# Attention maxima as two 64-row matmuls into a double bank, column-tiled sums, and a fixed VectorE order

## The chip, the cores and the metric

The kernel runs on one core of a Trainium2 chip. The metric is the device time in microseconds (us) of one execution, lower is better. A core has five engines that work in parallel, each through its own queue in order: TensorE (PE in the profile; PEld is its weight load), VectorE (DVE), ScalarE (ACT), GpSimd (POOL), and SyncE (SP), which here issues the transfers. TensorE writes into PSUM, which has 8 banks of 128 partitions by 512 floats; VectorE and ScalarE read it from there.

## What is computed

One layer of a transformer block on 2048 tokens of width 1024, with 256 context tokens. The part that the change touches is the attention: 8 query heads of 64 columns, 2 key/value heads (four query heads share one), and 2304 keys (256 context, 2048 latent) for every query.

```
def attend(q, k, v):
    s = jnp.einsum('bkgqd,bknd->bkgqn', q, k, preferred_element_type=jnp.float32)
    p = jax.nn.softmax(s, axis=-1).astype(v.dtype)
    return jnp.einsum('bkgqn,bknd->bkgqd', p, v)
```

Around it stand an input projection with norms and rotary tables, a gated MLP branch, a merge of the two branches with an output projection, and a squared-ReLU MLP.

## The kernel before, in words

The stages run one after another: the input projection (`project`, to about 782 us of the trace), the attention (`attend`, 782 to about 1545 us), the merge, and the MLP (`ffn`).

**Units.** `attend` (L890) goes over 16 units, one for each of 4 blocks of 512 queries and 4 pairs of heads. In a unit it goes over 18 key tiles of 128 keys in 3 groups of 6; the text calls them g0, g1 and g2, with key tiles j0 to j5, j6 to j11, j12 to j17. For each key tile `scores` (L810) makes the transposed scores of the two heads: two matmuls per head (L815, L816) into one bank, of 512 columns each, and an Exp on ScalarE (L818) into an SBUF tile. L815 multiplies the rounded queries with the keys (128 rows: the high and the low part of the keys). L816 adds the low part of the queries and, through a row of ones in `KB`, minus the maximum of the query. After the six key tiles of a group `values` (L821) is called for the six tiles of the group before it, so each group's values come one group later: two matmuls per key tile, one per head, each into its own 64 partitions of one bank `o` (L826, 64 weight columns; in the records each of these float32 matmuls appears as two instructions). The same function adds the exponentials up for the softmax sums, 8 additions of a unit on VectorE and the rest on GpSimd (L841).

**Maxima.** The maximum of a query must be known before its unit begins. `attn_prep` (L747) of the next unit is a generator that `attend` advances three times per key tile. It transposes the queries (L754, copied by L758), makes for each head, each of four 128-query tiles and each of five key blocks (one of 256 and four of 512 keys) one matmul into one bank (L770) and one maximum on VectorE (L774), 40 of each in a unit; then the maximum over the blocks (L779), its negative into the tile `pb` (L780), and the transposes of `pb` (L789, in the trace under the helper's line L161), which the next unit's L816 needs. `attn_load` (L731) fetches the queries of the unit after that and splits them (L740 to L742).

**Sums.** When a unit is over, `sums` (L844) adds the partial sums of GpSimd and VectorE (L846) and stores the unscaled output. `finish` (L853) then makes the row sums with 8 matmuls of one column (L858), 16 instructions in the records, a reciprocal (L863), a transpose (L866), and stores the result. `br_inputs` (L945) of the merge reads these reciprocals back, spread over 64 partitions, and multiplies (L962).

**Other work in the stage.** `mod_rest` (L273) goes over 32 weight tiles in 36 steps: each loads a tile and multiplies and adds on VectorE (L283, L287), and every ninth ends with some matmuls (L299, L315). `br_inputs(0)`, called `late` in `attend`, is handed out in the last unit, one step per key tile.

**What sets the order.** The source order is a priority; a scheduler at compile time places each engine's instructions by readiness in its own model. Two lists restrict it, both through `order` (L1393): the steps of `mod_rest` in `attend` are pinned on all engines to their place in the source, and TensorE's whole order in `attend` is that of the source (`pe_pins`). VectorE, ScalarE, GpSimd and SyncE may otherwise be reordered. PSUM is one pool of 8 banks for the whole kernel (L168); a bank is taken for each score tile, maximum, transpose and sum, and `o` holds one for most of a unit.

Of the kernel before, what the change touches and what calls it, by code (L numbers as in the profile page):

```python
# [9 lines left out]
F32 = mybir.dt.float32  # L10
# [51 lines left out]
class Kern:  # L62
    def __init__(self, ctx, tc, I, out):
# [5 lines left out]
        self.pe_pins = []  # L69
        self.open_pools, self.pool_of = {}, {}  # L70

# [91 lines left out]
    def constants(self):  # L163
# [4 lines left out]
        self.psp = ec(self.tc.tile_pool(name="ps", bufs=8, space=PSUM))  # L168
# [26 lines left out]
        def operands(n):  # L195
# [535 lines left out]
    def attn_load(self, b, p):  # L731
# [8 lines left out]
        nc.gpsimd.memset(pb[:, :, :, HD:], 0.0)  # L740
        nc.scalar.copy(pa, qt.unsqueeze(3).broadcast_to([P, TT, 2, 2, HD]))
        nc.vector.tensor_tensor(  # L742
            out=pb[:, :, :, :HD], in0=qt, in1=f32(pa[:, :, :, 0, :]), op=ALU.subtract
# [3 lines left out]
    def attn_prep(self, b, p, loaded, out):  # L747
# [17 lines left out]
        for h in range(2):  # L765
            for t in range(TT):
                for c, ka in enumerate(self.KA):
                    n = CTX if c == 0 else TB
                    ps = self.bank([TB])
                    nc.tensor.matmul(  # L770
                        ps[:, :n], qa[h][:, t * P : (t + 1) * P], ka[kv][:, :n],
                        start=True, stop=True,
                    )
                    nc.vector.tensor_reduce(  # L774
                        out=mx[:, t, h, c : c + 1], in_=ps[:, :n], axis=AX.X, op=ALU.max
                    )
                    yield
# [3 lines left out]
            out=pb[:, :, :, HD : HD + 1], in0=nm.unsqueeze(3), scalar1=-1.0, scalar2=None,  # L781
# [14 lines left out]
    def attn_steps(self, b, p, qab):  # L796
# [56 lines left out]
        def finish():  # L853
            sm = self.bank([2 * TT])
            for h in range(2):
                for t in range(TT):
                    c = h * TT + t
                    nc.tensor.matmul(  # L858
                        sm[:, c : c + 1], accs[1][h][:, t * P : (t + 1) * P],
                        self.ones[:, :1], start=True, stop=True,  # L860
                    )
            r = self.small([2 * TT])
# [27 lines left out]
    def attend(self, qabs, prep0, loaded, side, late):  # L890
# [5 lines left out]
        for i, u in enumerate(units):  # L896
# [4 lines left out]
            for g in range(0, NKT, GROUP):  # L901
# [14 lines left out]
                for f in pend:  # L916
                    f()
# [539 lines left out]
```

## Time and profile before

| what | us |
|---|---|
| median of 3 runs (lowest, highest) | 3280.03 (3278.81, 3280.11) |
| the profiled execution, its own time | 3275.92 |
| its span, first to last instruction | 3274.1 |
| attention: first score matmul of the first unit to that of the last (15 units) | 782.2 to 1499.9 |
| last unit, to its last value matmul | 1499.9 to about 1540 |

The profile is of one execution. A row of a list of groups gives the line, the engine, the operation, what it writes and reads, the shapes and the count; then the busy time and the mean duration of one; then the idle time ahead of it and what ended that. A row of a timeline gives start, duration, engine, line and, in brackets, the idle time before it and the instruction that ended it; `x3` means three merged instructions. TensorE is pipelined: a matmul of 512 columns lasts about 0.39 us in the records, but the next one starts before it ends, so the cost of one is the step from start to start. A row of a table by stretch gives the stretch and its length, the busy time of each engine with its number of instructions, the granted TensorE clock (1.00 is full), the share of DMA time, and GB/s.

### The profile page before, as it was taken

To read this page: it belongs to the slowest core of one execution; us is meant where nothing else is said; L and a number is where in the kernel's file an instruction comes from. 1 tells how busy PE (TensorE), PEld (TensorE's weight loads), DVE (VectorE), ACT (ScalarE), POOL (GpSimd) and SP (SyncE) were. 2 spreads that over 40 slices of the span, in tenths; PEclk is the share of its full clock that TensorE was granted. 3 is DMA by queue.
4 is the path that set the end of the run, shared out by engine and by line. 5 is a ranking of instruction groups with operands and counts; after the bars stand their busy time and mean duration, and the time that the engine had idled before them with its cause. 6 is when DMAs were issued, how large, how long until landed. Compare 5 with 4: busy or idle time off the path is not lost.

```text
span 3274.1 us, 38611 instructions
## 1 busy us (share of the span) xinstructions
PE 3127.4 (96%) x14100; PEld 2397.0 (73%) x14100; DVE 1987.0 (61%) x2910; ACT 1353.3 (41%) x2034; POOL 982.9 (30%) x672
## 2 busy tenths in 40 slices
PE   8999999999999999998799988999999899999999
PEld 4888887887555666664587766888778688888777
DVE  4736354556787888774433339887754676664555
ACT  3343534343444544453322216444543344443333
POOL 1423233334777887777633310000000000000000
PEclk9999999999999999999899998999999999999999
DMA  6353534342111111001555536989655634445564
GB/s 201 98 193 107 169 118 152 114 139 83 49 49 52 46 33 52 26 11 43 183 177 173 163 111 228 313 308 312 220 202 197 220 137 158 145 149 195 209 218 170
DMA packets 331838, 484.79 MB, mean 148 GB/s; under 512 B 33920, under 2 KB 166144, under 8 KB 331648
## 3 DMA queue, kind: packets, MB, share of 16 engines
q1 hardware_dynamic: 326032, 481.98, 44.0%
q8 instruction: 110, 1.80, 0.2%
q10 hardware_dynamic: 5616, 0.35, 0.1%
q14 instruction: 80, 0.66, 0.1%
HBM read 347.97 MB, written 134.28 MB: 147 GB/s over the span
## 4 chain that ended last, share of the span: by engine, by line
PE 76%; DVE 10%; DMA 5%; POOL 3%; issue 3%; ACT 2%; SPq 1%; ACTq 0%; DVEq 0%; POOLq 0%
PE b L1176 11%; PE b L1177 11%; PE b L1175 11%; PE b L157 7%; PE b L156 7%; PE b L155 7%; PE b L826 7%; PE b L770 4%; PE b L815 3%; PE b L816 3%; DVE ts L774 2%; PE b L161 2%; DMA f<-w2o_d 1%; DMA w<-in_w_in 1%; DVE f L1270 1%
## 5 line engine op out<-in xcount | busy, mean ns | idle before, releaser
L774 DVE TENSOR_REDUCE ts<-b 128x1 f32<-128x512 f32 (+1 forms) x640 | 357.4, 627 | 153.5 <-PE b L770 153.3
L841 POOL TENSOR_TENSOR t<-t,pt 128x512 f32<-128x512 f32 x272 | 376.5, 1410 | 137.2 <-ACT pt L818 134.6
L1261 DVE TENSOR_TENSOR f<-f,f 128x1024 fp32r<-128x1024 f32 x224 | 272.8, 1224 | 235.1 <-ACT f L1260 230.7
L1260 ACT CAST f<-f 128x1024 fp32r<-128x1024 f32 x224 | 235.0, 1051 | 381.8 <-DMA f<-ao_d 287.7
L1176 PE MATMUL b<-f,f 128*128 128x512 f32 x896 | 354.1, 395 | 15.2 <-DVE f L1261 14.7
L1177 PE MATMUL b<-h,f 128*128 128x512 f32 x896 | 350.0, 391 | 9.1 <-DVE f L1132 7.2
L1175 PE MATMUL b<-h,f 128*128 128x512 f32 x896 | 350.3, 392 | 4.8 <-ACT f L1131 4.3
L818 ACT ACTIVATE pt<-b 128x512 f32<-128x512 f32 x480 | 257.9, 603 | 227.0 <-PE b L816 221.7
L1177 PE MATMUL b<-f,f 128*128 128x512 f32 x896 | 351.1, 392 | 0.0
L1176 PE MATMUL b<-h,f 128*128 128x512 f32 x896 | 349.9, 391 | 0.0
L1175 PE MATMUL b<-f,f 128*128 128x512 f32 x896 | 306.6, 396 | 22.2 <-ACT f L1260 20.6
L127 POOL TENSOR_TENSOR w<-w,w 128x1024 fp32r<-128x1024 f32 x60 | 146.8, 2447 | 388.3 <-ACT w L123 152.0
L815 PE MATMUL b<-t,t 128*128 128x512 f32 x576 | 238.1, 413 | 0.0
L816 PE MATMUL b<-t,t 128*128 128x512 f32 x576 | 226.8, 394 | 0.0
L826 PE MATMUL b<-pt,t 128*64 128x512 f32 x960 | 223.3, 613 | 0.0
L123 ACT CAST w<-w 128x1024 fp32r<-128x1024 f32 x120 | 125.9, 1049 | 225.7 <-DMA w<-in_w_in 197.9
L1175 PEld LDWEIGHTS b<-f,f 128*128 128x128 f32 x896 | 168.7, 190 | 64.5 <-ACT f L1260 26.0
L1176 PEld LDWEIGHTS b<-f,f 128*128 128x128 f32 x896 | 169.8, 189 | 59.8 <-DVE f L1261 25.0
L155 PE MATMUL b<-t,w 128*128 128x512 f32 x512 | 203.2, 397 | 1.0 <-DVE t L568 1.0
L1177 PEld LDWEIGHTS b<-h,f 128*128 128x128 f32 x896 | 169.0, 189 | 45.9 <-DVE f L1132 7.9
L157 PE MATMUL b<-t,w 128*128 128x512 f32 x512 | 200.6, 392 | 0.0
L156 PE MATMUL b<-t,w 128*128 128x512 f32 x512 | 200.6, 392 | 0.0
(212 smaller groups left out, 6249.4 us busy)
## 6 DMA issues: line engine op xcount, KB each, us to landing
w<-in_w_in SPq DMA_DIRECT2D x120, 512.0 KB
ao_d<-f SPq DMA_DIRECT2D x224, 256.0 KB
f<-ao_d SPq DMA_DIRECT2D x112, 512.0 KB
f<-w2o_d SPq DMA_DIRECT2D x112, 512.0 KB
f<-in_w_ff SPq DMA_DIRECT2D x48, 1024.0 KB
w2o_d<-f SPq DMA_DIRECT2D x112, 256.0 KB
t<-in_w_mod SPq DMA_DIRECT2D x32, 512.0 KB
f<-x_d SPq DMA_DIRECT2D x64, 256.0 KB
```

Of the source, the lines that this page charges most:

```text
L155: mm(ps, sh, mh, start=start, stop=False)
L156: mm(ps, sh, ml, start=False, stop=False)
L157: mm(ps, sl, mh, start=False, stop=stop)
L774: nc.vector.tensor_reduce(out=mx[:, t, h, c : c + 1], in_=ps[:, :n], axis=AX.X, op=ALU.max)
L815: nc.tensor.matmul(s, self.KA[c][kv][:, ks], qa[h], start=True, stop=False)
L816: nc.tensor.matmul(s, self.KB[c][kv][:, ks], qb[h], start=False, stop=True)
L826: nc.tensor.matmul(o[0][h * HD : (h + 1) * HD, :], self.V[c][:, i, kv * HD : (kv + 1) * HD], pts[j][h], start=j == 0, stop=j == NKT - 1,)
L841: engs[e].tensor_tensor(out=accs[e][h], in0=first, in1=pt, op=ALU.add)
L1175: mm(ps, wh, hh, start=start and k == 0, stop=False, skip_group_check=True)
L1176: mm(ps, wh, hl, start=False, stop=False, skip_group_check=True)
L1177: mm(ps, wl, hh, start=False, stop=k == len(w) - 1, skip_group_check=True)
L1261: nc.vector.tensor_tensor(out=l, in0=f32(l), in1=f32(h), op=ALU.subtract)
```

## The change

Seven things are altered, all in or around `attend`.

1. The two heads' maxima are two matmuls of 64 rows, in rows 0 to 63 and 64 to 127 of the array, each into one half of a tile of two banks, `bb`. Both use only the high part of the keys; for that the halves of `KB` and of `pb` change places, so that the high part of the keys lies in rows 64 to 127 as well. One VectorE instruction takes both maxima: 20 of 2x512 or 2x256 numbers instead of 40.
2. The maxima come in bursts of two pairs, every fourth step of the generator, so 10 bursts in a unit. At three steps per key tile they stand behind j1, j3, j4 and j5, then j7, j8, j9 and j11, then j12 and j13.
3. PSUM in the attention is 4 single banks and 2 double ones; before and after it, 8 single ones. In the first unit's preparation, which runs within the projection, the pairs use two single banks and two maxima.
4. The sums are two matmuls with 64 columns of ones as weights and the 512 sums as moving operand, one for each half of the partitions; the row is copied by ScalarE and stored. After the fourth pair of heads of a block one transfer reads all 32 rows of 128 sums back, one reciprocal is taken, and one transfer stores it.
5. `finish` runs behind the values of g0 (that is, at the end of g1) and g1 instead of in the midst of the scores.
6. The steps of `mod_rest` move from behind j2, j8 and j14 to the ends of g0 and g2, with a second step at each in every fourth unit; `attn_load` moves from j11 to the end of g1. None is pinned.
7. VectorE's order in `attend` is that of the source, as TensorE's is (`fixed`).

```diff
--- before.py
+++ after.py
@@ -111,11 +112,28 @@
     def small(self, shape, dtype=F32):
         return self.sb("fs" if "back" in self.open_pools else "ts", shape, dtype)
 
-    def bank(self, shape, dtype=F32):
+    def psum(self, banks):
+        if self.banks:
+            self.psum_stack.close()
+        self.banks = banks
+        self.psum_stack = ExitStack()
+        self.psp = self.psum_stack.enter_context(
+            self.tc.tile_pool(name="ps", bufs=1, space=PSUM, reuse_waits="tile")
+        )
+
+    def bank(self, shape, dtype=F32, tag="b"):
         self.uid += 1
-        t = self.psp.tile([P] + list(shape), dtype, tag="b", name=f"b_{self.uid}")
-        self.tags[t.name] = "b"
+        t = self.psp.tile(
+            [P] + list(shape), dtype, tag=tag, name=f"{tag}_{self.uid}", bufs=self.banks[tag]
+        )
+        self.tags[t.name] = tag
         return t
+
+    def pair(self):
+        if "bb" in self.banks:
+            t = self.bank([2, TB], tag="bb")
+            return t, [t[:, i] for i in range(2)]
+        return None, [self.bank([TB]) for _ in range(2)]
 
     def split(self, src, hi, lo, hi_eng="act", lo_eng="pool"):
         nc = self.nc
...
@@ -203,13 +221,8 @@
 
         self.ao_d = [operands(f"ao{blk}") for blk in range(2)]
         self.wo_d = operands("w2o")
-        self.rs_d = [
-            [
-                dp.tile([2 * TT, P], F32, tag=f"rs{b}_{p}", name=f"rs_d{b}_{p}")
-                for p in range(NH // 2)
-            ]
-            for b in range(NB)
-        ]
+        self.sm_d = spill("sm", [NH, TB])
+        self.rs_d = spill("rs", [NH, TB])
         self.open("base")
         self.open("front")
 
...
@@ -762,23 +775,32 @@
         yield
         kv = p // 2
         mx = self.small([TT, 2, len(self.KA)])
-        for h in range(2):
-            for t in range(TT):
-                for c, ka in enumerate(self.KA):
-                    n = CTX if c == 0 else TB
-                    ps = self.bank([TB])
+        for t in range(TT):
+            tok = slice(t * P, (t + 1) * P)
+            for c, (ka, kb) in enumerate(zip(self.KA, self.KB)):
+                n = CTX if c == 0 else TB
+                both, ps = self.pair()
+                for h, (rows, k) in enumerate(((slice(0, HD), ka), (slice(HD, P), kb))):
                     nc.tensor.matmul(
-                        ps[:, :n], qa[h][:, t * P : (t + 1) * P], ka[kv][:, :n],
-                        start=True, stop=True,
+                        ps[h][:, :n], qa[h][rows, tok], k[kv][rows, :n], start=True, stop=True
                     )
+                if both is not None:
                     nc.vector.tensor_reduce(
-                        out=mx[:, t, h, c : c + 1], in_=ps[:, :n], axis=AX.X, op=ALU.max
+                        out=mx[:, t, :, c : c + 1], in_=both[:, :, :n], axis=AX.X, op=ALU.max
                     )
-                    yield
+                else:
+                    for h in range(2):
+                        nc.vector.tensor_reduce(
+                            out=mx[:, t, h, c : c + 1], in_=ps[h][:, :n], axis=AX.X,
+                            op=ALU.max,
+                        )
+                if (t * len(self.KA) + c) % 2:
+                    for _ in range(4):
+                        yield
         nm = self.small([TT, 2])
         nc.vector.tensor_reduce(out=nm, in_=mx, axis=AX.X, op=ALU.max)
         nc.vector.tensor_scalar(
-            out=pb[:, :, :, HD : HD + 1], in0=nm.unsqueeze(3), scalar1=-1.0, scalar2=None,
+            out=pb[:, :, :, 0:1], in0=nm.unsqueeze(3), scalar1=-1.0, scalar2=None,
             op0=ALU.mult,
         )
         for _ in range(6):
...
@@ -851,38 +873,42 @@
             nc.sync.dma_start(self.at_d[b][p * P : (p + 1) * P, :], oc)
 
         def finish():
-            sm = self.bank([2 * TT])
+            sm = self.bank([TB])
             for h in range(2):
-                for t in range(TT):
-                    c = h * TT + t
-                    nc.tensor.matmul(
-                        sm[:, c : c + 1], accs[1][h][:, t * P : (t + 1) * P],
-                        self.ones[:, :1], start=True, stop=True,
-                    )
-            r = self.small([2 * TT])
-            nc.vector.reciprocal(r, sm)
+                nc.tensor.matmul(
+                    sm[h * HD : (h + 1) * HD, :], self.ones[:, :HD], accs[1][h],
+                    start=True, stop=True,
+                )
+            row = self.t2([TB])
+            nc.scalar.copy(row, sm)
+            for h in range(2):
+                nc.sync.dma_start(
+                    self.sm_d[b][2 * p + h : 2 * p + h + 1], row[h * HD : h * HD + 1]
+                )
+            if p + 1 == NH // 2:
+                n = NH * TT
+                r = self.t1([P])
+                pack = lambda d: d.rearrange("h (t c) -> (h t) c", c=P)
+                nc.sync.dma_start(r[:n], pack(self.sm_d[b]))
+                yield
+                nc.vector.reciprocal(r[:n], r[:n])
+                nc.sync.dma_start(pack(self.rs_d[b]), r[:n])
             yield
-            rt = self.bank([P])
-            nc.tensor.transpose(rt[: 2 * TT], r, self.ident)
-            rr = self.t1([P])
-            nc.scalar.copy(rr[: 2 * TT], rt[: 2 * TT])
-            nc.sync.dma_start(self.rs_d[b][p], rr[: 2 * TT])
-            yield
 
         return scores, values, sums, finish
 
     def kb_build(self):
         nc = self.nc
         z = self.t2([TB])
-        nc.gpsimd.memset(z[HD:], 0.0)
-        nc.gpsimd.memset(z[HD : HD + 1], 1.0)
+        nc.gpsimd.memset(z[:HD], 0.0)
+        nc.gpsimd.memset(z[0:1], 1.0)
         for c, KA in enumerate(self.KA):
             n = TB if c else CTX
             KB = []
             for ka in KA:
                 kb = self.t2([TB], F32R)
-                nc.vector.tensor_copy(kb[:HD, :n], f32(ka[:HD, :n]))
-                nc.scalar.copy(kb[HD:, :n], z[HD:, :n])
+                nc.vector.tensor_copy(kb[HD:, :n], f32(ka[:HD, :n]))
+                nc.scalar.copy(kb[:HD, :n], z[:HD, :n])
                 KB.append(kb)
                 yield
             self.KB.append(KB)
...
@@ -903,18 +929,18 @@
                     scores(j)
                     for _ in range(3):
                         next(prep, None)
-                    if j % 6 == 2:
-                        at = self.here()
-                        next(side, None)
-                        self.pins.append(range(at, self.here()))
-                    if j in (GROUP + 4, 2 * GROUP + 1):
-                        next(after, None)
-                    if j == 11 and i + 2 < len(units):
-                        loaded.append(self.attn_load(*units[i + 2]))
                     if i + 1 == len(units):
                         next(late, None)
                 for f in pend:
                     f()
+                if g:
+                    next(after, None)
+                if g == GROUP and i + 2 < len(units):
+                    loaded.append(self.attn_load(*units[i + 2]))
+                else:
+                    next(side, None)
+                    if i % 4 == 0:
+                        next(side, None)
                 pend = [lambda v=values, j=j: v(j) for j in range(g, g + GROUP)]
             for _ in prep:
                 pass
...
@@ -928,7 +954,7 @@
             pass
         for _ in side:
             pass
-        self.pe_pins.append(range(begin, self.here()))
+        self.fixed.append(range(begin, self.here()))
 
     def load_w_out(self):
         nc = self.nc
...
@@ -990,6 +1015,7 @@
         for _ in start:
             pass
         self.close("mid", "base")
+        self.psum({"b": 8})
         self.open("join")
         steps = [(b, m) for b in range(NB) for m in range(KC)]
         it = iter(steps)
...
@@ -1379,7 +1405,10 @@
 
         prep0 = tail()
         self.project(prep0)
+        for _ in prep0:
+            pass
         self.close("front")
+        self.psum({"b": 4, "bb": 2})
         self.open("mid")
         self.open("pre", side="right")
         first = {}
...
@@ -1403,7 +1433,7 @@
                 if n in self.tags and n not in seen:
                     seen.add(n)
                     keys.append(self.tags[n])
-            held = idx in pinned or (idx in pe and i.engine == tensor)
+            held = idx in pinned or (idx in fixed and i.engine in engines)
             after = keys + ([i.engine] if held else [])
             for prev in {last[k].name for k in after if k in last}:
                 self.tc.add_manual_dep(i, prev, dep, reason="order")
```

Left out: the halves in `attn_load` exchanged in the same way as in `kb_build`, the reads of `rs_d` in `br_inputs` in the new layout, the first `self.psum({"b": 8})`, and the renaming in `__init__`.

More of the change, by code (lines that the diff above doesn't have):

```diff
@@ L68, in __init__ @@
         self.pins = []
-        self.pe_pins = []
+        self.fixed = []
         self.open_pools, self.pool_of = {}, {}
+        self.banks = None
     def here(self):
@@ L1390, in build @@
         self.close("back")
+        self.psum_stack.close()
         self.order()
```

17 lines of the change are left out of this document (8 added, 9 removed).

## The prediction

> **What bounds the kernel now.** I read the page first, then the table by stretches, the groups of the attention stage, and TensorE's timeline start by start.
>
> ```profile
> span 3274.1 us, 38611 instructions
> ...
> PE 3127.4 (96%) x14100; PEld 2397.0 (73%) x14100; DVE 1987.0 (61%) x2910; ACT 1353.3 (41%) x2034; POOL 982.9 (30%) x672
> ...
> PE   8999999999999999998799988999999899999999
> ...
> DVE  4736354556787888774433339887754676664555
> ...
> PEclk9999999999999999999899998999999999999999
> ```
>
> TensorE is busy nearly everywhere; in the attention, slices 10 to 19, VectorE is at 70 to 80% beside it. Where TensorE is full, time is won only by taking work or waits from it. The stage by stretches (columns: PE, PEld, DVE, ACT, POOL, clock):
>
> ```profile
> 782.20:1499.90 717.70, 701.87 (x3255) 433.98 (x3253) 578.10 (x830) 347.47 (x651) 551.87 (x401) 0.98 0.13 41
> ...
> 1408.90:1454.40 45.50, 45.26 (x219) 28.61 (x217) 34.17 (x53) 22.96 (x43) 34.68 (x27) 1.00 0.04 13
> ```
>
> The first row is 15 units: 47.85 us each. The second is one unit with no `mod_rest` step at full clock: 45.5 us, so TensorE's own work. The difference, 717.7 - 15 x 45.5 = 35.2 us, is other matmuls and lost time. So two questions decide: what the change does to the 45.5, and how much of the 35.2 goes.
>
> The groups of the stage:
>
> ```profile
> L774 DVE TENSOR_REDUCE ts<-b 128x1 f32<-128x512 f32 x480 | 301.2, 680 | 111.4 <-PE b L770 111.3
> L841 DVE TENSOR_TENSOR t<-t,pt 128x512 f32<-128x512 f32 x80 | 99.5, 1243 | 13.4 <-ACT pt L818 11.4
> L841 DVE TENSOR_TENSOR t<-pt,pt 128x512 f32<-128x512 f32 x32 | 53.6, 1676 | 0.0
> L287 DVE SCALAR_TENSOR_TENSOR t<-t,silu,t 128x1024 f32<-128x1024 f32 x28 | 50.6, 1808 | 0.0
> L774 DVE TENSOR_REDUCE ts<-b 128x1 f32<-128x256 f32 x120 | 49.7, 414 | 28.9 <-PE b L770 28.9
> L858 PE MATMUL b<-ones,t 128*128 128x1 f32 x240 | 28.3, 248 | 0.0
> L841 DVE TENSOR_TENSOR t<-t,t 128x512 f32<-128x512 f32 x16 | 12.9, 807 | 0.7
> L299 PE MATMUL b<-t,ones 128*128 128x512 f32 x8 | 3.8, 592 | 0.0
> L315 PE MATMUL b<-ones,t 128*128 128x1 f32 x32 | 3.7, 245 | 0.0
> ```
>
> **TensorE's part of a unit.** The steps from start to start:
>
> ```profile
> 1417.62 0.63 PE L770 MATMUL b<-t,t 128*128 128x512 f32 x2
> 1418.18 1.08 PE L826 MATMUL b<-pt,t 128*64 128x512 f32 x4
> ...
> 1422.52 1.03 PE L826 MATMUL b<-t,t 128*64 128x512 f32 x4
> 1423.48 0.50 PE L815 MATMUL b<-t,t 128*128 128x512 f32 x1
> 1423.81 0.39 PE L816 MATMUL b<-t,t 128*128 128x512 f32 x1
> ...
> 1426.70 0.39 PE L815 MATMUL b<-t,t 128*128 128x512 f32 x1
> 1426.92 0.39 PE L816 MATMUL b<-t,t 128*128 128x512 f32 x1
> ...
> 1427.60 0.73 PE L770 MATMUL b<-t,t 128*128 128x512 f32 x3
> 1428.18 0.40 PE L815 MATMUL b<-t,t 128*128 128x512 f32 x1
> ```
>
> A step of 512 columns is 0.23 us (1426.70 to 1426.92), a key tile's four score matmuls 0.92. The three L770 from 1427.60, one of 256 columns, take 0.58 = 0.23 + 0.11 + 0.23. So the 40 maxima of a unit take 32 x 0.227 + 8 x 0.113 = 8.2 us. Taken two at a time they are 20 steps: **-4.1 us**. That two such tiles run together is seen here for 64-column tiles: the four L826 from 1422.52 end after 1.03, two steps of 0.43 with two instructions in each.
>
> Against it stands the change of mode. From full to 64 columns: the last L770 starts at 1417.85, the first L826 at 1418.18, which is 0.33 where 0.23 is usual, and the next pair starts 0.05 late (four end after 1.08, not 1.03): 0.15 us. Back: the last pair starts at 1422.95, L815 at 1423.48, 0.52 where 0.43 is usual, and L816 comes 0.33 after it, not 0.23: 0.21 us. No row shows 64-row tiles. The bounds are 0 and this; I take this, the only change of mode that the trace has. Ten bursts cost 10 x 0.36 = 3.6, less 2 x 0.21 where a burst ends a group (behind j5 and j11) and values follow anyway: **+3.2 us**. So most of what pairing wins goes into the modes. The Trainium skill (TensorEngine Tiling (Array Packing), Key Properties) states that changing the tiling mode drains the TensorE; the trace agrees, with 0.10 us lost at each of the two changes before the weight load comes on top.
>
> The sums: 16 one-column instructions (28.3 / 240 x 16 = 1.9 us) become 4 in two steps of 0.43, right behind the values in the same mode: **-1.0 us**. In total -1.9 us.
>
> **VectorE and the two double banks.** VectorE's maximum lasts 0.680 for 512 numbers and 0.414 for 256, so 1.04 ns per number: 1.21 us for 2x512 (estimate). In a row they overlap by (480 x 0.680 - 301.2) / 480 = 0.05, so one comes every 1.16. Two double banks hold two pairs, so a burst's second pair waits for the second maximum of the burst before.
>
> ```profile
> 1204.59 0.85 PE L770 MATMUL b<-t,t 128*128 128x512 f32 x3
> ...
> 1205.02 5.21 DVE L774 TENSOR_REDUCE ts<-b 128x1 f32<-128x512 f32 x9 [1.66 <-PE b L770]
> ```
>
> From first matmul to first maximum is 0.43. So the second maximum is over 0.43 + 1.16 + 1.21 = 2.80 us after the burst's first matmul, and handing the bank back takes 0.14 at most (818.76 to 818.90 in a row below), of which I take half. TensorE, with one key tile between, wants the bank 0.23 + 0.23 + 0.21 + 0.92 + 0.15 + 0.23 = 1.97 after it. The wait of 0.9 occurs three times in a unit, behind j4, j8 and j13, where two full pairs lie one key tile back (elsewhere there are two key tiles between, or a short pair): **+2.7 us**. Eight banks hid this before.
>
> Four single banks, one of them `o`:
>
> ```profile
> 1500.70 5.01 ACT L818 ACTIVATE pt<-b 128x512 f32<-128x512 f32 x10 [5.33 <-PE b L816]
> ```
>
> ScalarE makes one exponential per 0.49 us (10 in 5.01), TensorE one score tile per 0.46. Behind j14 to j17, without maxima between, TensorE loses 8 x 0.03: **+0.2 us** (0 to 0.6). A unit comes to 45.5 - 1.9 + 2.7 + 0.2 = 46.5 us; 15 of them: **+15 us**.
>
> **What goes of the 35.2 us.** L299 and L315 are 7.5 us and stay. The other 27.7 are waits and half-clock stretches:
>
> ```profile
> 818.90 1.94 PE L161 MATMUL b<-ident,t 128*128 128x128 f32 x8 [3.00 <-DVE t L780]
> ```
> ```profile
> 976.68 0.62 ACT L123 CAST in<-raw 128x512 fp32r<-128x512 f32 x1 [7.74 <-DVE raw L962]
> ...
> 978.81 0.58 PE L770 MATMUL b<-t,t 128*128 128x256 f32 x1 [2.31 <-ACT t L758]
> ```
> ```profile
> 1146.00:1149.40 3.40, 3.18 (x22) 2.66 (x22) 3.40 (x7) 1.22 (x3) 3.40 (x3) 1.00 0.00 0
> 1149.40:1152.80 3.40, 3.40 (x9) 1.07 (x10) 3.40 (x7) 1.09 (x2) 3.32 (x3) 0.50 0.01 2
> ```
>
> The first: an addition was put between L779 and L780, and the transposes of `pb` waited; in source order L780 follows L779. The second: `br_inputs`, meant for the last unit, was moved up; ScalarE waited 7.74 us for VectorE's L962 with the queries' copies behind it. With VectorE's order fixed, L962 cannot come before the last unit. The third: 3.4 us at half clock behind a stretch with the 16 one-column matmuls of L858, which go. I leave 3.4 us for half clock elsewhere: **-24.3 us**.
>
> **What is added at the edges.** First the second `mod_rest` step of every fourth unit.
>
> ```profile
> 1409.96 1.03 PE L161 MATMUL b<-ident,t 128*128 128x128 f32 x8
> 1410.75 0.48 PE L815 MATMUL b<-t,t 128*128 128x512 f32 x1
> ```
>
> On TensorE g0's scores last 6 x 0.92, plus 0.8 for the transposes, plus the bursts with their modes, 0.70, 0.82, 0.70 with a wait of 0.9, and 0.61: 10.1 us from the unit's start; its values, 12 steps of 0.43, and the mode bring it to 15.5. VectorE begins the last two maxima at 9.6 + 0.43 and is free at 12.3; three additions (166.0 / 128 = 1.3 us each) bring it to 16.2, a step of 1.8 to 18.0. The first maximum of g1 is wanted at 15.5 + 2 x 0.92 + 0.1 + 0.43 = 17.9. There is no slack, so the second step adds 0 to 1.8 us; I take 1.0, four times: **+4 us**. In the last unit VectorE has only additions beside `br_inputs`, whose transfers now hold those up in line, 0 to 5 us; I take **+1**. At the end:
>
> ```profile
> 1544.89 0.28 SPq L869 DMA_DIRECT2D rs_d<-t  x1
> 1545.27 0.38 SPq L974 DMA_DIRECT2D bw<-in_w_br_attn  x1
> ...
> 1547.91 0.62 ACT L123 CAST bw<-bw 128x512 fp32r<-128x512 f32 x1 [3.04 <-DMA bw<-in_w_br_attn]
> ```
>
> The merge's loads stand behind the store of the last sums on SP. Now that queue may hold a store, a load and a store in a chain, 0 to 5 us at about 2 us for each that waits for the one before (the load at 1545.27 ended ScalarE's wait at 1547.91); the shorter sums give 1 back: **+1**. The same chain after the three other blocks has g2 to run in. In the projection, streaming and mode cost nearly cancel: 0.
>
> **Sum:** 15 - 24.3 + 4 + 1 + 1 = -3.3 us on the profiled execution's 3275.9, which gives 3272.6. The median of the runs lies 4.1 above that execution, so **3277 us**, 0.1% below 3280.0.
>
> **The rivals.**
>
> *The change of mode is cheap for row tiles* (faster). Then 3.2 us of a unit go, but bursts come 0.36 sooner and each of three waits grows by that: -2.1 us a unit, -32 in all: 3245. For it: nothing measured speaks on row tiles. Against it: both changes in the trace cost. The Trainium skill (TensorE: Matmul & The Clock Gate, Packing small matmuls) says that a weight load overlaps running matmuls only when row groups differ; full and half tiles share rows, so it speaks against this rival too, and no row here tests it.
>
> *VectorE becomes the bound behind the values* (slower). A first maximum of g1 has no slack, so whatever makes VectorE later there is paid by TensorE one for one. Additions vary from 0.81 to 1.68 us by group. If the three ahead of g1 and the step take 0.5 us longer each through GpSimd's load, with nothing free to be moved up in their place, a unit gets 1.5 us longer: +22: 3299. It decides from about 0.8 us per unit on. Against it: the 1.3 us are already a mean over contended ones.
>
> *The pairs do not run at once* (slower; the change would not do what it says). Streaming stays 8.2: +4.1, the three waits shrink by 0.45 each: +2.8 a unit, +42: 3319. Against it: column tiles do run together.
>
> **How the numbers follow.** The forecast has 0.47, cheap modes 0.28, VectorE 0.17, no pairing 0.08. About 0.2% (6.6 us) can be told from no change. The forecast's own range, from the bounds of edges, half clock and banks, is 3263 to 3293: it gives 0.17 to faster, 0.19 to same, 0.11 to slower. With the rivals: faster 0.45, same 0.19, slower 0.36. The range 3238 to 3308 takes in the first two rivals and leaves out the third and some of the first.
>
> **What would show it.** Starts within a pair of L770's successor a few ns apart, or 0.23 (third rival). Steps into and out of a burst 0.15 and 0.21 longer, or not (first rival). Unstalled units of 46.5 us; TensorE waiting for VectorE's maximum about 0.9 us behind j4, j8 and j13; a longer wait at j8 means the second rival. No half-clock stretch where the sums are, and no wait of 2 us for copies or `pb`. The forecast is wrong if a unit lies outside 44 to 48, or if the 27.7 us are not the fixed order's to win.

## The result, and the profile after

The changed kernel takes **3375.24 us** (median of 4 runs, 3372.41 to 3380.28) where the kernel before, beside it, takes 3279.42: a ratio of 1.030, 95% interval 1.028 to 1.032. The forecast was 3277, with a range that ended at 3308. It is wrong in sign and in size.

The page of the changed kernel, the rows that were shown of before:

```profile
span 3375.5 us, 37968 instructions
...
PE 3144.3 (93%) x13892; PEld 2323.0 (69%) x13892; DVE 1981.3 (59%) x2598; ACT 1359.1 (40%) x2034; POOL 990.9 (29%) x672
...
PE   7999999999898989889689996999999999999998
...
PEclk9999999999998989999899997999999999999999
```

No engine has much more to do: VectorE is busy 6 us less than before and TensorE 17 us more, on 208 fewer instructions, part of them at a lower clock. What is new are the 8s and 6s of TensorE in slices 10 to 20, the attention, with dips of the clock beside them. So it looks like waiting, not work.

The changed kernel's 15 units in the table by stretches (us, then PE, PEld, DVE, ACT, POOL, clock, share of DMA, GB/s):

```profile
783.10:1576.30 793.20, 711.60 (x3073) 367.26 (x3073) 544.44 (x506) 349.95 (x644) 553.82 (x399) 0.94 0.10 32
```

They last 793.2 us where the row of before had 717.7, so **+75.5**; VectorE is busy 34 us less and the clock averages 0.94, not 0.98: 0.06 x 793 = 48 us of clock are missing, where 0.02 x 718 = 14 us were missing before. From the first score matmul of the last unit to the first matmul of the merge it is 72.8 us where it was 53.3, **+19.5**. The rest of the kernel adds 6. These two numbers, units and last unit, are what each experiment below is read by.

What TensorE and VectorE wait for (engine, what it needs <- who gives it: total us, times, longest):

```profile
PEld bb L784 <- DVE ts L788: 126.2, 122, 4.5
DVE t L755 <- ACT t L754: 97.4, 13, 7.8
```

TensorE waits for maxima, as long as 4.5 us, and VectorE itself waits 13 times, about 7.5 us each, for ScalarE's cast of the queries in `attn_load`: once in almost every unit. One such place, VectorE's timeline at the end of g1:

```profile
1070.68 1.82 DVE L788 TENSOR_REDUCE ts<-bb 128x2 f32<-128x1024 f32 x2 [0.39 <-PE bb L784]
1072.42 1.12 DVE L863 TENSOR_TENSOR t<-pt,pt 128x512 f32<-128x512 f32 x1
1081.02 1.71 DVE L755 TENSOR_TENSOR t<-t,t 128x512 f32<-128x512 f32 x1 [7.48 <-ACT t L754]
1082.65 4.61 DVE L788 TENSOR_REDUCE ts<-bb 128x2 f32<-128x1024 f32 x4
```

ScalarE and TensorE at the same time:

```profile
1076.98 0.59 ACT L883 COPY t<-b 128x512 f32<-128x512 f32 x1 [6.00 <-PE b L878]
1077.60 1.13 ACT L840 ACTIVATE pt<-b 128x512 f32<-128x512 f32 x2
1079.46 0.60 ACT L840 ACTIVATE pt<-b 128x512 f32<-128x512 f32 x1 [0.73 <-PE b L838]
1079.95 1.04 ACT L754 CAST t<-t 128x1024 fp32r<-128x1024 f32 x1
```
```profile
1077.97 0.73 PE L784 MATMUL bb<-t,t 64*128 64x512 f32 x4
...
1079.43 0.39 PE L838 MATMUL b<-t,t 128*128 128x512 f32 x1
1083.92 0.79 PE L784 MATMUL bb<-t,t 64*128 64x512 f32 x2 [4.10 <-DVE ts L788]
1085.05 0.80 PE L784 MATMUL bb<-t,t 64*128 64x512 f32 x2 [0.34 <-DVE ts L788]
1085.78 0.79 PE L837 MATMUL b<-t,t 128*128 128x512 f32 x1
1086.37 0.63 PE L838 MATMUL b<-t,t 128*128 128x512 f32 x1
```

It reads as a chain. The subtraction L755 stands in the source at the end of g1, so VectorE's fixed order puts it ahead of the maxima of j12 and j13. Its cast L754 is made by ScalarE, whose order is not fixed, behind L883 and three exponentials of g2. L883 is the copy of the row of sums that items 4 and 5 of the change put there; it waits 6.00 us for the values and the sums. The load of the queries had gone out at 1062.00, and no transfer runs from 1066 to 1072, so the trace shows nothing else that kept the cast from running in these 6 us. VectorE waits for it; TensorE's pairs of 1077.97 fill both double banks; the next pair has no bank and TensorE stops for 4.10 us. Then its matmuls last 0.63, not 0.39. The same stretch in the table (after the length: PE, PEld, DVE, ACT, POOL, clock, share of DMA, GB/s):

```profile
1079.60:1083.00 3.40, 0.22 (x1) 0.00 (x0) 1.98 (x2) 1.89 (x3) 3.24 (x4) 0.80 0.74 287
1083.00:1086.40 3.40, 2.14 (x6) 1.10 (x7) 3.40 (x4) 0.00 (x0) 3.32 (x4) 0.50 0.00 0
1086.40:1089.80 3.40, 3.40 (x12) 2.48 (x10) 3.30 (x5) 2.22 (x5) 2.51 (x4) 0.69 0.00 0
```

A stretch with TensorE busy for 0.22 us is followed by half clock (0.50) until 1088.5. The Trainium skill (TensorE: Matmul & The Clock Gate, What's actually happening) says that an idle window of about 3.4 us halves the clock and a busy one restores it; the trace agrees, a wait of 4.10 us and half clock after it. In four of the 13 units the wait is shorter than that, 3.08 to 3.21 us, and half clock follows there as well (0.57 to 0.60 from the end of the wait to the transposes of `pb`).

### The profile page after: what moved, and what is told of

The parts are those of the page before. It is cut to its first block, busy times and chain, and to the rows that moved or that the text cites. A ratio compares the mean times of both kernels' runs of the same rounds, so it can differ in the third digit from the quotient of the medians.

```text
span 3375.5 us, 37968 instructions
## 1 busy us (share of the span) xinstructions
PE 3144.3 (93%) x13892; PEld 2323.0 (69%) x13892; DVE 1981.3 (59%) x2598; ACT 1359.1 (40%) x2034; POOL 990.9 (29%) x672
## 4 chain that ended last, share of the span: by engine, by line
PE 72%; DVE 12%; DMA 6%; POOL 4%; issue 3%; ACT 3%; SPq 1%; ACTq 0%; DVEq 0%; POOLq 0%
PE b L1202 11%; PE b L1203 11%; PE b L1201 11%; PE b L175 7%; PE b L173 6%; PE b L174 6%; PE b L848 6%; PE b L837 4%; PE b L838 3%; DVE ts L788 3%; PE bb L784 2%; PE b L179 2%; DMA f<-w2o_d 1%; DMA w<-in_w_in 1%; DVE f L1296 1%
## 5 line engine op out<-in xcount | busy, mean ns | idle before, releaser
L788 DVE TENSOR_REDUCE ts<-bb 128x2 f32<-128x512 f32 x300 | 318.6, 1112 | 139.8 <-PE bb L784 139.6
L837 PE MATMUL b<-t,t 128*128 128x512 f32 x576 | 268.8, 467 | 4.3 <-ACT pt L840 3.5
L838 PE MATMUL b<-t,t 128*128 128x512 f32 x576 | 242.9, 422 | 0.0
L173 PE MATMUL b<-t,w 128*128 128x512 f32 x512 | 202.9, 396 | 1.5 <-DVE t L581 1.4
L784 PE MATMUL bb<-t,t 64*128 64x256 f32 x600 | 123.8, 466 | 81.6 <-DVE ts L788 81.6
L175 PE MATMUL b<-t,w 128*128 128x512 f32 x512 | 199.8, 390 | 0.0
```

The lines of the kernel that those rows point to most:

```text
L173: mm(ps, sh, mh, start=start, stop=False)
L175: mm(ps, sl, mh, start=False, stop=stop)
L788: nc.vector.tensor_reduce(out=mx[:, t, :, c : c + 1], in_=both[:, :, :n], axis=AX.X, op=ALU.max)
L837: nc.tensor.matmul(s, self.KA[c][kv][:, ks], qa[h], start=True, stop=False)
L838: nc.tensor.matmul(s, self.KB[c][kv][:, ks], qb[h], start=False, stop=True)
```

## The experiments

**Theory after this reading:** the wait of VectorE at L755 is the loss in the units, half clock included; the last unit is longer because `br_inputs` and the chain of the last sums stand ahead of what the merge needs. **Rivals:** the fixed order as such; row tiles or double banks.

All kernels in one table; "units" and "last" are the two stretches named above, from each kernel's trace; "before" is the median of the kernel before, run beside it. From the merge to the end it is 1718 to 1728 us in every kernel.

| kernel | units | last | median | before | ratio (95%) |
|---|---|---|---|---|---|
| before | 717.7 | 53.3 | 3280.03 | | |
| after | 793.2 | 72.8 | 3375.24 | 3279.42 | 1.030 (1.028 to 1.032) |
| sub_late | 714.8 | 72.5 | 3292.83 | 3280.97 | 1.005 (1.003 to 1.006) |
| cast_early | 786.5 | 71.8 | 3361.64 | 3275.24 | 1.027 (1.024 to 1.029) |
| ve_free | 760.2 | 55.8 | 3321.20 | 3280.97 | 1.012 (1.011 to 1.014) |
| before_fixed | 743.6 | 71.4 | 3329.65 | 3280.97 | 1.015 (1.013 to 1.017) |
| sub_late_full | 722.6 | 72.6 | 3303.33 | 3280.97 | 1.007 (1.005 to 1.008) |
| sub_late_loose | 735.2 | 54.7 | 3293.45 | 3275.24 | 1.006 (1.004 to 1.008) |
| loose_chain | 727.8 | 51.5 | 3284.55 | 3275.24 | 1.003 (1.002 to 1.004) |
| loose_banks8 | 692.0 | 59.8 | 3257.43 | 3275.24 | 0.995 (0.993 to 0.997) |
| late_spread | 715.4 | 61.0 | 3281.50 | 3273.81 | 1.002 (1.000 to 1.003) |
| best | 693.9 | 56.6 | 3261.65 | 3273.81 | 0.995 (0.993 to 0.997) |
| best_full | 679.8 | 56.5 | 3249.37 | 3273.81 | 0.991 (0.988 to 0.994) |

### sub_late: only the subtraction moved

```diff
                 if g:
                     next(after, None)
+                if g == 2 * GROUP and i + 2 < len(units):
+                    self.sub()
                 if g == GROUP and i + 2 < len(units):
-                    loaded.append(self.attn_load(*units[i + 2]))
+                    loaded.append(self.attn_load(*units[i + 2], defer=True))
```

`attn_load` loads and casts where it did; its subtraction, now `self.sub`, is issued a group later.

> The changed kernel with one instruction moved: VectorE's subtraction of attn_load (L755) is issued at the end of g2, behind the maxima and the values, instead of at the end of g1; the load, the cast on ScalarE (L754) and the memset stay. Theory (a wait in the fixed order): in the changed kernel L755 stands in VectorE's fixed line ahead of g2's first maxima and waits for ScalarE's L754, which stands behind g2's first exponentials; TensorE waits 4.2 us for the maxima in 13 units, and the clock halves behind that. Then about 13 x 4.3 = 56 us of waits and some 30 us of half clock go: near 3290 us, units of 46 to 48 us. Rival (VectorE's work itself is too much behind the values): the maxima of g2 stay late, units stay above 52 us, time above 3350 us. Rival (modes and double banks): as the first rival, the units stay long but spread over g0 and g1 too.

The units go from 793.2 to 714.8, and the clock comes back:

```profile
783.40:1498.20 714.80, 679.92 (x3072) 341.01 (x3072) 551.49 (x506) 345.14 (x644) 552.81 (x399) 1.00 0.11 35
1211.60:1258.70 47.10, 45.10 (x207) 22.40 (x205) 38.52 (x35) 23.09 (x43) 38.59 (x28) 1.00 0.10 23
```

So one instruction of 1.4 us, placed a group too early, cost 78.4 us in the units, more than their whole loss. Of this, 76.9 us lie in g2 of the 13 units. From g2's first score matmul to the first pair of maxima behind j13 they take 6.1 to 7.1 us where sub_late takes 2.9: 49.5 us in all, the wait. From that pair to the transposes of `pb` they take 7.0 to 8.2 where sub_late takes 5.6: 27.2 us in all, at a granted clock of 0.57 to 0.76. The last unit does not change (72.5), and the kernel is 0.5% slower than the one before, no longer 3%, close to the 3290 expected. What the prediction took for the double banks is seen here as it was priced:

```profile
1074.81 0.40 PE L844 MATMUL b<-t,t 128*128 128x512 f32 x1
1075.17 0.50 PE L790 MATMUL bb<-t,t 64*128 64x512 f32 x2
1076.30 0.39 PE L790 MATMUL bb<-t,t 64*128 64x256 f32 x2 [0.63 <-DVE ts L794]
1076.62 0.50 PE L843 MATMUL b<-t,t 128*128 128x512 f32 x1
```

From 1075.17 to 1076.30 it is 1.13 where a pair takes 0.23: a wait of 0.90, behind j4.

### cast_early: the cast moved ahead instead

```diff
                 if g == GROUP and i + 2 < len(units):
-                    loaded.append(self.attn_load(*units[i + 2]))
-                else:
+                    self.sub()
+                if g == 0 and i + 2 < len(units):
+                    loaded.append(self.attn_load(*units[i + 2], defer=True))
+                if g != GROUP or i + 2 >= len(units):
                     next(side, None)
```

Load and cast stand at the end of g0, the subtraction stays at the end of g1.

> The changed kernel with VectorE's subtraction of attn_load left at the end of g1, but its load, cast (L754 of the changed kernel) and memset issued one group earlier, at the end of g0 (the mod_rest step stays at g0 and g2). Theory (VectorE's line waits for ScalarE's cast): the cast is over before g1 ends, VectorE does not wait, time within 6 us of sub_late (3293). Rival (the place of the subtraction in VectorE's line itself is what costs): it stays above 3350 us. A middle value would say that the cast still slips behind exponentials in some units.

It stays at 3361.64, a miss, and the most useful one. VectorE's timeline at the end of a g0:

```profile
1047.51 1.29 DVE L869 TENSOR_TENSOR t<-t,pt 128x512 f32<-128x512 f32 x2
1055.26 2.40 DVE L300 SCALAR_TENSOR_TENSOR t<-t,silu,t 128x1024 f32<-128x1024 f32 x1 [6.45 <-DMA t<-in_w_mod]
1057.58 2.94 DVE L794 TENSOR_REDUCE ts<-bb 128x2 f32<-128x1024 f32 x3
...
1070.34 1.76 DVE L756 TENSOR_TENSOR t<-t,t 128x512 f32<-128x512 f32 x1
```

The subtraction (L756) no longer waits. But now `mod_rest`'s L300 does, for its weights (64.8 us in 11 waits), which SP issues only at 1051.08, right behind a store of the unit before (L879, 1050.65). A g1 takes 22 to 25 us in these eleven units where it is 16.0 to 16.7 in most of sub_late. Another instruction and another giver, a group earlier, but again in VectorE's line ahead of the maxima, and nearly the same price. So the time is the one that the rival named, but the reason is not. In the two units with an early cast in which L300 does not wait, 3 and 10, the unit is as long as in sub_late (48.8 and 48.9 us): the subtraction in its old place then costs nothing.

### ve_free: only TensorE's order fixed

```diff
-        engines = (self.nc.tensor.engine, self.nc.vector.engine)
+        engines = (self.nc.tensor.engine,)
```

> The changed kernel with only TensorE's order fixed in the attention, as before the change; VectorE may be reordered by the scheduler. Theory (a wait in the fixed order): L755 no longer holds the maxima up, time near 3300 us (the moved-up br_inputs and additions ahead of the transposes may come back and cost some 10 to 20 us of that). Rival (modes and double banks cost the time): it stays above 3350 us.

At 3321.20 it lies between the theory's 3300 and the rival's 3350, and the units are at 760.2. The wait at L755 is gone, and TensorE waits for `pb`, and ScalarE for the transposes of it, far more than in the kernel before (there 5.4 us in 11 waits of PE at L161 for L780):

```profile
ACT t L813 <- PE b L179: 35.5, 18, 3.7
...
PE b L179 <- DVE t L802: 31.0, 13, 3.2
```

The last unit falls to 55.8: with VectorE free, `br_inputs` is again done before it.

### before_fixed: the kernel before with VectorE's order fixed

```diff
-            held = idx in pinned or (idx in pe and i.engine == tensor)
+            held = idx in pinned or (idx in pe and i.engine in engines)
```

> The kernel before with VectorE's order in the attention fixed to the source, and nothing else. Theory (a wait in the fixed order): L742 is issued behind j11's maxima and ahead of g0's additions and g2's maxima, and waits for L741 on ScalarE; it has TensorE's values of 5 us as slack, so it costs from 1 to 4 us a unit, plus half clock, and the last unit is held up by br_inputs as in the changed kernel: 3300 to 3350 us. Rival (the fixed order by itself is harmless or wins the waits that I had put on free order): 3245 to 3280 us.

The fixed order alone makes the kernel before 1.5% slower, and its last unit 71.4 long. The time lies in the range of the theory, but the wait that this named, L742 for L741, has no row in the trace. What the fixed order was to remove, the late `pb`, it makes worse (5.4 us in the kernel before for the first row here):

```profile
PE b L161 <- DVE t L780: 30.9, 11, 3.8
PEld b L161 <- DVE t L780: 27.8, 9, 4.2
...
DVE t L287 <- DMA t<-in_w_mod: 10.8, 7, 2.0
```

In source order `mod_rest`'s step behind j14 stands ahead of L779 and L780. It takes VectorE 1.3 to 2.4 us itself, and in seven units it waits for its weights too. So a fixed order is neither good nor bad; what counts is what stands ahead in it and when its data come.

### sub_late_full: 128 rows in the double banks

```diff
-                        ps[h][:, :n], qa[h][rows, tok], k[kv][rows, :n], start=True, stop=True
+                        ps[h][:, :n], qa[h][:, tok], ka[kv][:, :n], start=True, stop=True
```

> sub_late with the maxima taken by full matmuls of 128 rows (high and low part of the keys, as before the change), one after the other, into the same double banks and with the same single VectorE instruction: no change of mode. By the sum of the prediction the pairing wins 4.1 us of streaming and pays 3.2 to 4 us of modes in a unit, so this is within 1 us a unit of sub_late, 15 us in all, and the waits for the double banks get shorter by 0.1 us each. Rival (cheap modes): 40 us slower than sub_late.

The units take 722.6, 7.8 more than with pairs: pairing wins 0.5 us a unit here, of the 4.1 that it saves in streaming, as expected; the rival of cheap modes would be 40 us.

### sub_late_loose and loose_chain: the last unit

```diff
+                        at = self.here()
                         next(late, None)
+                        self.loose.update(range(at, self.here()))
...
-        fixed = {n for r in self.fixed for n in r}
+        fixed = {n for r in self.fixed for n in r} - self.loose
```

`br_inputs`' instructions are free on VectorE again; loose_chain, besides, issues the last unit's `sm_d` stores, its load and its `rs_d` store on ScalarE's queue (`queue = nc.scalar`).

> sub_late with the VectorE instructions of br_inputs in the last unit left free in order. Theory (in the last unit VectorE's additions stand behind br_inputs' transfers, GpSimd's sums wait for these, and the merge starts 19 us later than before, counted from the last unit's start): the stretch from the last unit to the merge falls from 72.5 to 56 to 60 us, in all 13 to 17 us less than sub_late; if the scheduler moves br_inputs up into earlier units again, their units pay 2 to 4 us each of it back, three or four of them. Rival (the delay is the chain of store, load, reciprocal and store at the end): 72 us stay.

> sub_late_loose with the last unit's store of the sums, load, and store of the reciprocals issued from ScalarE's queue instead of SP's, so that the merge's loads do not stand behind them. Theory (that chain delays the merge's loads): 3 to 4 us less than sub_late_loose. Rival (the loads are held by something else, such as space): no difference.

The last stretch falls by 17.8, to 54.7, and by another 3.2 on ScalarE's queue. What the chain delays is read in the changed kernel's SP timeline:

```profile
1636.80 0.51 SPq L885 DMA_DIRECT2D sm_d<-t  x2
1638.29 0.31 SPq L892 DMA_DIRECT2D t<-sm_d  x1
1640.81 0.31 SPq L895 DMA_DIRECT2D rs_d<-t  x1
1641.16 0.42 SPq L999 DMA_DIRECT2D bw<-in_w_br_attn  x1
```

The merge's first load goes out 4.4 us behind the first store of the chain, and 64.9 us behind the unit's start where it was 45.4 in the kernel before. But in sub_late_loose the units pay 20.4, so that in all nothing is won over sub_late, a miss. They pay it for two reasons. Freed, `br_inputs` is moved up into units 0 and 5, which get 4.6 and 6.9 us longer, with waits of 6.14 and 3.57 us for maxima; the same two units are as long in loose_chain. Units 13 and 14 are 4.9 and 2.8 longer for another reason, which loose_chain does not have: one VectorE addition in each lasts 8.56 and 7.57 us (more on these below). That is why loose_chain's units are 7.4 us shorter; its queues differ in the last unit only.

### loose_banks8: 8 single banks

```diff
-        self.psum({"b": 4, "bb": 2})
+        self.psum({"b": 8})
```

Two maxima per pair then, on sub_late_loose.

> sub_late_loose with eight single banks in the attention instead of four and two double ones: the row pairs go into two single banks and VectorE takes two maxima. Theory (three waits of 0.9 us per unit for the second double bank): they go, 15 x 2.7 = 40 us less than sub_late_loose, units of 44.4 us. Rival (VectorE is short of time anyway, with 40 maxima again instead of 20): less than 10 us.

The units take 692.0, 43 less, and the kernel is the first that beats the one before. The three waits of 0.9 would be 2.7 x 15 = 40.5 of that; some 8 of the 43 are the two long additions, which this kernel does not have, and what the other kernels with 8 banks show (below) is less.

### late_spread, best, best_full

```diff
-                    if i + 1 == len(units):
-                        next(late, None)
                 for f in pend:
                     f()
+                if 3 * i + g // GROUP >= 31:
+                    next(late, None)
```

late_spread is sub_late with `br_inputs` kept in the fixed order, but cut into load, multiply with cast, and subtraction, one or two parts at each group end from unit 10 on. best adds 8 banks and ScalarE's queue for the last sums; best_full is best with maxima of 128 rows.

> sub_late with br_inputs' eight steps taken out of the last unit: each is cut into load, multiply with ScalarE's copy, and subtraction, and these parts stand one after the other at the group ends from the second group of unit 10 on, still in VectorE's fixed order, so that no instruction of VectorE follows at once on a transfer or a copy that it needs. Theory (the last unit is long because VectorE's fixed line waits there for the transfers of br_inputs, with the additions behind it): the stretch from the last unit's start to the merge falls from 72.5 to 55 us, as in sub_late_loose, while the 15 units stay at about 715 us, unlike in sub_late_loose: near 3275 us, no difference to the kernel before. Rival (VectorE has no room at the group ends): four multiplies and eight subtractions are 8 us and are paid in the units: near 3283. Rival (the length of the last unit comes from the chain of the last sums alone): 72 us stay, near 3293.

> late_spread with 8 single banks in place of 4 single and 2 double ones (two maxima instructions per pair), and with the last unit's store, load and store of the sums on ScalarE's queue. If the parts add up: 36 us less for the banks (sub_late_loose 3293.5 to loose_banks8 3257.4), 3 us less for the queue: near 3236 us, 1.2% faster than the kernel before; 15 units of 45 us, 677 to 690 us, and about 52 us from the last unit to the merge. Rival (40 single maxima keep VectorE so long that the added parts of br_inputs do not fit): units of 47, near 3265.

> best with the maxima as two matmuls of 128 rows one after the other, as before the change; all else the same. It tells what pairing itself is worth where nothing waits for a bank. If pairing wins the prediction's 4.1 us a unit and pays 0.40 us at each of eight bursts that are not at a group's end, 3.2: 0.9 us a unit, 13 us, so 13 us slower than best (near 3249 if best is at 3236). Rival (modes cost little and sub_late_full was held by its banks): 4 us a unit, 60 us slower than best. Rival (all ten bursts pay, or more than 0.40): the same time as best or less.

late_spread: the units keep 715.4, so the parts cost nothing there, and the last stretch falls from 72.5 to 61.0, not to 55; GpSimd's additions end 45.1 us behind the unit's start (1544.3) where it was 41.3 in sub_late_loose, which is 3.8 of the 6. best, at 3261.65, is no faster than loose_banks8: the 8 banks take 21.5 us from the units (715.4 to 693.9), not 36, a miss. best_full is the fastest, 0.9% under the kernel before, and 12 us under best, where 13 us over it was expected; the last rival, the same time or less, is what came. Here pairing loses. A full burst in best, from the last score matmul ahead of it:

```profile
1158.38 0.39 PE L844 MATMUL b<-t,t 128*128 128x512 f32 x1
1158.70 0.73 PE L790 MATMUL b<-t,t 64*128 64x512 f32 x4
1159.36 0.50 PE L843 MATMUL b<-t,t 128*128 128x512 f32 x1
1159.70 0.39 PE L844 MATMUL b<-t,t 128*128 128x512 f32 x1
```

and in best_full:

```profile
1147.67 0.39 PE L844 MATMUL b<-t,t 128*128 128x512 f32 x1
1147.90 1.07 PE L790 MATMUL b<-t,t 128*128 128x512 f32 x4
1148.81 0.39 PE L843 MATMUL b<-t,t 128*128 128x512 f32 x1
1149.03 0.39 PE L844 MATMUL b<-t,t 128*128 128x512 f32 x1
```

1.32 against 1.36 us from the first row to the last. Two pair steps of 0.23 stand for four single ones, but the entry takes 0.32 (1158.38 to 1158.70) and the step after leaving 0.34 (1159.36 to 1159.70) where 0.23 is usual, and the two pairs with their way out 0.66, not 0.46: 0.40 in all. What is won, 0.04, turns into a loss in a burst with a tile of 256, which saves 0.11 less. And TensorE reaches the banks sooner than VectorE hands them back; TensorE's weight loads waiting for maxima in best, then in best_full:

```profile
PEld b L843 <- DVE ts L799: 20.5, 56, 2.4
```
```profile
PEld b L843 <- DVE ts L799: 8.4, 12, 2.5
```

A unit without a stall, best and best_full:

```profile
1108.10:1153.20 45.10, 44.85 (x206) 23.30 (x206) 34.03 (x53) 22.98 (x43) 34.58 (x27) 1.00 0.14 48
```
```profile
1098.00:1142.50 44.50, 44.50 (x207) 27.16 (x206) 34.34 (x53) 22.86 (x43) 34.80 (x27) 1.00 0.14 48
```

That is 0.6 us. Between all 15 units it is 14.1 us, and 8.5 of these are in units 1 and 5 of best, which stall. VectorE and TensorE of best in unit 1:

```profile
851.14 9.32 DVE L869 TENSOR_TENSOR t<-pt,pt 128x512 f32<-128x512 f32 x1
```
```profile
861.12 1.39 PE L790 MATMUL b<-t,t 64*128 64x512 f32 x3 [2.43 <-DVE ts L799]
```

One addition lasts 9.32 us, where the same one lasts 0.85 in best_full; the maxima behind it come late, and half clock follows. Unit 5 has another of 9.30. Nothing here shows that the pairs have a part in this, so what pairing itself loses in this trace is the other 5.6 us, 0.4 a unit.

## Why the prediction was wrong, step by step

**The step that failed: "What goes of the 35.2 us".** It counted what VectorE's fixed order removes and never what it adds. Item 6 of the change moves `attn_load` to the end of g1, item 7 fixes its subtraction there; nothing in the sum or the rivals priced the wait of L755 for ScalarE's cast, nor asked what ScalarE has ahead of that cast (L883, by items 4 and 5) and what is queued behind L755 on VectorE. It was 78.4 us (after to sub_late): 49.5 up to the end of 13 waits of TensorE for maxima, 3.1 to 4.1 us each, and 27.2 in the stretch at lower clock behind them. The second rival came near, VectorE late for the maxima, but at the first maximum of g1, by VectorE's own work, and at 22 us; the long wait came behind j13, not behind j8.

**With that wait gone, the sum for the units holds.** By its own terms it was 717.7 + 15 - 24.3 + 4 = 712.4; sub_late has 714.8. Part of that agreement is luck: 15 plain units came 9.0 us over the sum (47.1 for 46.5), and the rest, 8.3 us, came 6.6 under the 14.9 that it left for other matmuls, half clock and `mod_rest`. In its parts:
- Pairs run together, right: the two matmuls of a pair start 0.003 us apart.
- Modes: 0.40 us for a burst where 0.36 was taken; row tiles pay as column tiles do, and the first rival falls. So of the 4.1 us won by streaming a unit kept 0.5 with double banks and lost 0.4 to 0.6 with 8 banks.
- Three waits of 0.90 us for the second double bank: right, seen behind j4, j8 and j13; behind j8, where the first pair of the burst is the short one, it is 1.0. With 8 banks a unit without a stall goes from 47.1 to 45.1 (sub_late, best), so 2.0 of the 2.7 come back.
- The plain unit: 47.1 against 46.5, the 0.04 of eight bursts being half of it.
- The sums: best_full has 128-row maxima and 8 banks as the kernel before, and its unit without a stall is 44.5 against 45.5, which agrees with the 1.0 taken. The sums were not run alone.
- The waits and half clock: 0.98 granted before, 1.00 in sub_late, right on the condition that nothing late stands in the line; in after it was the other way round.
- The second `mod_rest` step: g1 is 2.1, 0.6 and 0.7 longer in units 4, 8 and 12, about the 1.0 taken.

**The second step that failed: the last unit, "+1" and "+1".** They measured 17.8 (sub_late to sub_late_loose) and 3.2 (to loose_chain). The transfers were bounded with 0 to 5 us for all; each of four multiplies waits by itself for its load:

```profile
DVE raw L987 <- DMA raw<-rs_d: 13.6, 4, 4.5
DVE in L145 <- ACT in L141: 6.5, 6, 3.2
```

That is 20 us in line ahead of the additions which GpSimd needs for the last sums, and these stand on SP ahead of the merge's loads.

**What stays open.** Why an addition of VectorE at times lasts 5 to 9 us. Most of the difference between the two figures for 8 banks, 43 and 21.5 us, comes from it: without units 13 and 14 of the one pair of kernels and units 1 and 5 of the other, 8 banks win 2.5 and 2.1 us a unit. Not tried were where the other 0.7 of the 2.7 us for the banks goes, and whether it is enough to put the cast ahead of L883.

## What to carry to other kernels

Before an engine's order is fixed, go through its list and ask of each instruction when its last input comes, from which engine or queue, and who is served behind it; one that waits ahead of work that frees PSUM banks is paid by TensorE, and a wait that leaves TensorE idle for 3 to 4 us is paid again in clock (here 27 us on top of 49). Move the late consumer first: it was enough in sub_late, while in cast_early, where its producer was moved, another late instruction held up the same line. Tiles of 64 rows between full ones had to win more than 0.4 us a burst here before they won anything.

## What was unexpected in the hardware

- Behind a wait of 4.10 us TensorE's matmuls ran at half clock from 1083.9 to 1088.5: one late instruction on VectorE, once a unit, took the mean clock of 793 us to 0.94.
- Tiles of 64 rows cost 0.20 us at a change of mode in each direction; 64-column tiles cost 0.15 and 0.21 in the kernel before.
- One maximum over two banks of 512 lasts 1.22 us, and 20 of them over two double banks served TensorE worse than 40 single ones over 8 banks: a unit without a stall is 47.1 us with the 20 (late_spread) and 45.1 with the 40 (best).
- A VectorE addition or subtraction of 512 columns, mostly 0.7 to 1.8 us in the attention, lasted 5.2 to 9.3 us nine times in the traces of five of the thirteen kernels. GpSimd, with additions of about 1.3 us, worked through all of them: in best from before 851.14 to 859.91 without a gap, then one of 0.08 us, and VectorE's addition ended at 860.46. That the one held up the other is a guess; no experiment here tests it.
